# Bias tables of a neighbourhood attention loaded once per group in one transfer, into two buffers, a group ahead

## The chip, the core and the metric

The kernel runs on one core of a Trainium2 chip. The metric is the device time in microseconds (us) of one execution. The engines named below are TensorE (PE in the profile, its weight loads PEld), VectorE (DVE), ScalarE (ACT), GpSimd (POOL) and SyncE (SP). SP computes nothing here: it is the queue from which nearly all DMA transfers are issued, in a fixed order, each of them after the waits that it carries.

## What is computed

The program is a two-layer backbone over 1024 latent tokens (a grid of 16 rows by 64 columns) with 256 context tokens ahead of them. The first layer has two attentions, the second a convolution and a 2-D neighbourhood attention. The change lies in this second attention:

```python
bias = rpb[:, dr_idx][:, :, dc_idx] + col_mask[None, None]
bias = jnp.transpose(bias, (0, 2, 1, 3)).reshape(D_HEADS, GRID_W, kh * GRID_W)
bias = jnp.concatenate([ctx_open, bias], axis=-1)[None, :, None]
kk = jnp.concatenate([c_dk, kr], axis=1)
vv = jnp.concatenate([c_dv, vr], axis=1)
return gqa_attend(qr[:, :, :, None, :], kk, vv, bias).reshape(bsz, GRID_W, D_W)
```

Each of the 16 query rows sees a window of 8 key rows by 16 columns and the whole context; a learned table of relative positions is added to the scores. There are 8 heads of 64 channels. The host lays the table out for each head as additive tables with a large negative number where a key is outside the window.

## The kernel before

**Groups.** The second attention works in 16 groups: 8 heads times 2 halves of the grid's columns (`hf`; a half is 32 query columns by 16 rows, so 512 queries, and the 40 key columns that they can see, so 640 keys). `SEQ` sets the order of the groups: both halves of heads 0 to 5, then half 0 of heads 6 and 7, then half 1 of both. Below, group n is the n-th of this order, counted from 0.

**Tiles.** A group has 7 tiles of 128 keys: context, five tiles of grid keys, context. Only some query rows reach a key tile (`QROWS`), so the tiles are 512, 256, 352, 512, 320, 224 and 512 queries wide. `attn_gen` does for each tile: two matmuls for the scores (`st`, L467 and L471, keys on partitions), for grid tiles the addition of the bias on VectorE (`pf<-st,bs`, L476), the exponential on ScalarE, a split into two parts `ph` (ScalarE) and `pl` (GpSimd or VectorE), and, three tiles later, three matmuls with the values (`ov`, L411 to L413). At a group's end VectorE normalises, and `y` goes to DRAM (`O1d`, L1382).

**Preparation.** Ahead of its tiles a group is prepared by `attn_prep`: its queries are loaded (`QH` twice, `QL`, L1307 to L1309), the row maxima of the scores are found (`maxes`: matmuls `mx`, L1351 and L1359, then VectorE over `mx`, L1353, and over `mx` plus a second bias table with queries on partitions, `bm`, L1360), and the negated maxima are transposed (`trn`, L389) into a row of `QL`. Group g+2 is prepared while group g runs: its load is written at the start of group g, its `mx` some tiles later.

**Bias tables.** `bs` is the table that L476 adds. It is loaded piece by piece, one transfer for each grid tile, three tiles ahead (`ahead`, L1326), into one buffer for the 512-wide piece and four for the others. `bm` is the table for the maxima: three pieces for a group (440, 320 and 320 columns, L1316) in two buffers (`BMB = 2`), so that the third waits until the first is read. Every piece is a transfer of its own on SP's queue.

**Other loads of a group.** At the start of the first half of a head the keys of the next head are loaded (`KAt`, two transfers of 384 KB, L363), at the start of each group its values (`Vt`, two transfers, L1337), in its middle a gate (`gt`, L1331). `KAt` waits until the last score tile of the group before has been read by TensorE.

**What is woven in.** `weave` runs the attention with other work in turns: the projections of heads 4 to 7 (`p`, L320 to L322, with weights `wr`), then the output projection (`po`). These matmuls fill TensorE between an attention's tiles. The order of instructions on each engine, SP among them, is then set by a list scheduler from priorities, buffers and its own estimate of when things are ready. On the chip each engine keeps that order, whatever arrives late.

Of the kernel before, what the change touches and what calls it, by code (L numbers as in the profile page):

```python
# [10 lines left out]
F32 = mybir.dt.float32  # L11
# [7 lines left out]
P = 128  # L19
# [8 lines left out]
NR, NW = 16, 40  # L28
NCOL = (0, 24)
QROWS = ((0, 8), (0, 11), (0, 16), (6, 16), (9, 16))  # L30
KROWS = ((0, 8), (0, 11), (4, 15), (8, 16))
BSO = (0, 256, 608, 1120, 1440)
BMO = (0, 320, 320, 760)
LOOK0, LOOK1 = 3, 3
LEAD = (3, 4)
AHEAD = 3
BMB = 2
CWB = 12
VSH = 5
VORD = (1, 2, 0)  # L40
# [49 lines left out]
def tile_kernel(ctx: ExitStack, tc: tile.TileContext, a, out):  # L90
    nc = tc.nc
    VE, SC, GP, PE, SY = nc.vector, nc.scalar, nc.gpsimd, nc.tensor, nc.sync
# [20 lines left out]
    def nm(s):  # L113
        uid[0] += 1
        return f"{s}_{uid[0]}"
# [538 lines left out]
    with ExitStack() as p0x:  # L654
# [231 lines left out]
        for k in range(4):  # L886
            u = ORDER[k]
            n = NSTEP[u // 2] + (12 if k == 0 else 0)
# [216 lines left out]
    with ExitStack():  # L1105
# [182 lines left out]
        dpool = ctx.enter_context(tc.tile_pool(name="d1", bufs=1, reuse_waits="tile"))  # L1288
# [7 lines left out]
        def load_head(hd):  # L1296
            i, e = divmod(hd, 2)
            ds = slice(e * 64, (e + 1) * 64)
            heads[hd] = load_k(hd, KD[i][ds])

        def group1(gi, hd, hf):
            i, e = divmod(hd, 2)
            ds = slice(e * 64, (e + 1) * 64)
            bms, bss = {}, {}

            def load_q(QH, QL):
                SY.dma_start(QH[0:64, :].bitcast(F32), QD[i][ds, 0, hf])  # L1307
                SY.dma_start(QH[64:128, :].bitcast(F32), QD[i][ds, 0, hf])
                SY.dma_start(QL[0:64, :].bitcast(F32), QD[i][ds, 1, hf])  # L1309
                for b in (1, 0, 3):  # L1310
                    load_bm(b)

            def load_bm(b):
                n = (KROWS[b][1] - KROWS[b][0]) * NW
                bms[b] = dpool.tile([P, 440], F32, tag="bm", name=nm("bm"), bufs=BMB)[:, :n]
                SY.dma_start(bms[b], a["d_bm"][hd, hf, :, BMO[b] : BMO[b] + n])  # L1316
                if b == 1:
                    bms[2] = bms[1]

            def ahead(t):  # L1320
                if g.tiles[t][3] is not None:
                    n = g.tiles[t][2]
                    t -= 1
                    w = dpool.tile([P, 512 if n > 352 else 352], F32, tag="bsl" if n > 352 else "bss", name=nm("bs"),
                                   bufs=1 if n > 352 else 4)
                    SY.dma_start(w[:, :n], a["d_bs"][hd, hf, :, BSO[t] : BSO[t] + n])  # L1326
                    bss[t] = w[:, :n]

            def gate():
                g.gt = half("gt1")  # L1330
                SY.dma_start(g.gt[ds], GD[i][ds, hf])  # L1331

            def start():
                if hf == 0 and hd < 7:
                    load_head(hd + 1)
                for j, k, n in ((0, 0, 2), (2, 2 + 5 * hf, 5)):
                    SY.dma_start(Vs[gi % 2][:, j : j + n, 0:128].bitcast(F32), VD[i][:, k : k + n, e])  # L1337
# [34 lines left out]
            def finish(ov, rb):  # L1372
# [6 lines left out]
                if i == 3:  # L1379
                    split(y[ds], od3[hf][ds, 0], od3[hf][ds, 1], "s", "v")  # L1380
                    return
                SY.dma_start(O1d[ds, i, hf], y[ds])  # L1382

            g = Group(load_q=load_q, maxes=maxes, nmp=2, bias=True, rate=3, ahead=ahead, sink=None, tiles=tiles, den=den, finish=finish,
                      start=start, gate=gate, last=last,
                      k=lambda: Ks[hd % len(Ks)], load_v=None, v=lambda k: Vs[gi % 2][:, k if k < 2 else k - 5 * hf, :])
            g.prep = attn_prep(kvp, g)
            return g

        SEQ = [(hd, hf) for hd in range(6) for hf in range(2)] + [(hd, hf) for hf in range(2) for hd in (6, 7)]  # L1390
        groups1 = [group1(gi, *x) for gi, x in enumerate(SEQ)]
        load_head(0)
        copy_k(*heads[0])
# [249 lines left out]
```

## Time and profile before

| | |
|---|---|
| median of 3 runs | 1566.65 us |
| lowest, highest | 1564.84, 1571.33 us |
| span of the profiled execution, first to last instruction | 1569.6 us |
| mean granted TensorE clock in it | 0.961 |
| PE busy in the span | 1460.8 us (93%) |
| DVE, POOL, ACT busy | 1129.4, 830.0, 762.0 us |
| moved by DMA | 221.03 MB, mean 141 GB/s |
| first matmul of the second attention | 1219.29 us after the span's start |

For the profiled execution the profile gives the span and no second time around it; it lies 2.95 us above the median, inside the runs' own spread. The second attention runs from about 1219 us to about 1535 us of the span. A row of a timeline gives start and duration, then in brackets how long the engine had stood idle just before it and what ended that. A row of waits gives, for who waited and whom for, the sum in us, how many times, and the longest. Sizes in KB are those of the profile (1024 bytes).

### The profile page before, as it was taken

Reading aid. Unit: us, or ns where it says so; the run is one execution under the profiler, and the core shown is the slowest. Engines: PE = TensorE matmul, PEld = TensorE weight load, DVE = VectorE, ACT = ScalarE, POOL = GpSimd, SP = SyncE. Lnnn points to the kernel's source line nnn. Section 1 sums busy time; section 2 is a strip of 40 time slices with the busy share of each in tenths; the row PEclk is TensorE's granted clock in tenths of the full one; section 3 lists DMA queues with packets and bytes.
Section 4 is the critical chain, followed back from the end, with each engine's and each line's share of the span. In section 5 each row is a group of like instructions: output and inputs, shape, how many; then the busy total and the mean of one; then the engine's idle time right before and its main releaser. Section 6 shows DMA issues by size and latency. Waiting matters only on the chain.

```text
span 1569.6 us, 22251 instructions
## 1 busy us (share of the span) xinstructions
PE 1460.8 (93%) x6984; PEld 1178.9 (75%) x6984; DVE 1129.4 (72%) x2172; ACT 762.0 (49%) x1545; POOL 830.0 (53%) x762
## 2 busy tenths in 40 slices
PE   6989999998999999899999889999999999899995
PEld 1878877876888677588887568888887787677784
DVE  4898896797768677455488668999654466776776
ACT  2721354545454754655555746443343445545472
POOL 1561463555465675756545756665443333444575
PEclk9899999999999999999999989999999999799897
DMA  9548245424431225612112022214547888889632
GB/s 337 190 142 260 87 142 167 132 67 125 154 116 47 67 91 167 224 47 61 48 38 85 14 94 61 81 58 148 177 154 224 237 229 242 248 231 251 187 95 108
DMA packets 199438, 221.03 MB, mean 141 GB/s; under 512 B 18956, under 2 KB 155352, under 8 KB 199320
## 3 DMA queue, kind: packets, MB, share of 16 engines
q1 hardware_dynamic: 192656, 208.04, 43.5%
q10 hardware_dynamic: 6664, 11.57, 2.3%
q8 instruction: 55, 0.90, 0.2%
q14 instruction: 63, 0.52, 0.1%
HBM read 159.51 MB, written 60.03 MB: 140 GB/s over the span
## 4 chain that ended last, share of the span: by engine, by line
PE 65%; DVE 14%; DMA 11%; issue 4%; POOL 2%; SPq 2%; ACT 1%; ACTq 0%; DVEq 0%; POOLq 0%
PE p L322 6%; PE p L321 6%; PE p L320 6%; PE ov L411 4%; PE ov L413 4%; PE ov L412 4%; PE po L320 4%; PE po L321 4%; PE po L322 4%; PE st L467 4%; PE st L471 4%; DMA mw<-in_mod_w_dram 3%; DVE macc L221 2%; PE pq L322 2%; PE pq L321 2%
## 5 line engine op out<-in xcount | busy, mean ns | idle before, releaser
L301 POOL TENSOR_TENSOR pl<-pf,ph 128x512 fp32r<-128x512 f32 (+4 forms) x321 | 393.7, 1237 | 320.1 <-ACT ph L298 260.0
L301 POOL TENSOR_TENSOR wl<-wr,wh 128x256 fp32r<-128x256 f32 (+2 forms) x256 | 197.5, 788 | 203.1 <-ACT wh L298 192.4
L479 ACT ACTIVATE pf<-st 128x512 f32<-128x512 f32 x284 | 167.3, 597 | 177.4 <-PE st L471 138.3
L298 ACT CAST ph<-pf 128x512 fp32r<-128x512 f32 (+4 forms) x364 | 210.5, 588 | 28.9 <-PE ov L412 21.5
L298 ACT CAST wh<-wr 128x256 fp32r<-128x256 f32 (+2 forms) x264 | 102.8, 404 | 172.9 <-DMA wr<-in_ev_qkv_dram 40.4
L320 PE MATMUL p<-hh,wh 128*128 128x512 f32 x448 | 177.5, 398 | 2.9 <-DVE spk L301 1.5
L321 PE MATMUL p<-hl,wh 128*128 128x512 f32 x448 | 178.0, 398 | 0.2 <-POOL hl L301 0.2
L322 PE MATMUL p<-hh,wl 128*128 128x512 f32 x448 | 175.9, 400 | 0.1
L467 PE MATMUL st<-QH,KAt 128*128 128x512 f32 (+4 forms) x364 | 145.4, 401 | 11.4 <-ACT pf L479 9.7
L411 PE MATMUL ov<-ph,Vt 128*128 128x512 f32 (+4 forms) x364 | 143.5, 394 | 9.7 <-ACT ph L298 5.0
L413 PE MATMUL ov<-pl,Vt 128*128 128x512 f32 (+4 forms) x364 | 144.1, 396 | 6.8 <-POOL pl L301 3.6
L471 PE MATMUL st<-QL,KBt 68*128 68x512 f32 (+4 forms) x364 | 139.0, 391 | 5.8 <-DVE QL L390 5.7
L412 PE MATMUL ov<-ph,Vt 128*64 128x512 f32 (+4 forms) x364 | 140.5, 386 | 0.0
L1122 DVE SCALAR_TENSOR_TENSOR cps<-U,taps,cps 128x512 f32<-128x512 f32 x184 | 124.3, 748 | 0.0
L591 DVE TENSOR_REDUCE mp<-mx 128x1 f32<-128x512 f32 x128 | 85.7, 682 | 42.5 <-PE mx L590 41.8
L221 DVE SCALAR_TENSOR_TENSOR macc<-mw,csil,macc 128x512 f32<-128x512 f32 x107 | 94.5, 901 | 17.5 <-DMA mw<-in_mod_w_dram 16.7
L320 PEld LDWEIGHTS p<-hh,wh 128*128 128x128 f32 x448 | 84.6, 189 | 23.6 <-DVE spk L301 1.7
L321 PEld LDWEIGHTS p<-hl,wh 128*128 128x128 f32 x448 | 84.5, 189 | 20.4 <-POOL hl L301 0.6
L322 PEld LDWEIGHTS p<-hh,wl 128*128 128x128 f32 x448 | 84.8, 189 | 20.1 <-POOL wl L301 0.6
L467 PEld LDWEIGHTS st<-QH,KAt 128*128 128x128 f32 x364 | 71.2, 196 | 33.4 <-ACT pf L479 17.6
L413 PEld LDWEIGHTS ov<-pl,Vt 128*128 128x128 f32 x364 | 71.1, 195 | 32.5 <-POOL pl L301 7.8
L411 PEld LDWEIGHTS ov<-ph,Vt 128*128 128x128 f32 x364 | 71.3, 196 | 27.3 <-ACT ph L298 8.4
(277 smaller groups left out, 3546.2 us busy)
## 6 DMA issues: line engine op xcount, KB each, us to landing
mw<-in_mod_w_dram SPq DMA_DIRECT2D x34, 512.0 KB, 5.9
Q<-qs SPq DMA_DIRECT2D x40, 256.0 KB, 2.7
QH<-Q SPq DMA_DIRECT2D x80, 128.0 KB, 2.8
wr<-in_od_d_dram SPq DMA_DIRECT2D x64, 128.0 KB, 2.7
mw<-in_mod_w_dram SPq DMA_DIRECT2D x28, 256.0 KB, 3.3
wr<-in_ev_qkv_dram SPq DMA_DIRECT2D x32, 192.0 KB, 3.6
KAt<-KD SPq DMA_DIRECT2D x16, 384.0 KB, 6.2
wr<-in_od_wo_dram SPq DMA_DIRECT2D x48, 128.0 KB, 3.2
```

The costliest lines, as they stand in the source:

```text
L221: VE.scalar_tensor_tensor(t, w, csil[:, dk, q : q + 1], t, op0=ALU.mult, op1=ALU.add)
L298: SC.copy(hi, src)
L301: (GP if leng == "g" else VE).tensor_tensor(lo, src, hi.bitcast(F32), op=ALU.subtract)
L320: PE.matmul(o, lh, rh, start=first, stop=False)
L321: PE.matmul(o, lh, rl, start=False, stop=False)
L322: done[0] = PE.matmul(o, ll, rh, start=False, stop=last)
L411: PE.matmul(o, V[:, 64:192], ph[:, :n], start=(t == 0), stop=False)
L412: PE.matmul(g.ov[0:64, q0 : q0 + n], V[:, 0:64], ph[:, :n], start=False, stop=False)
L413: pvs.append(PE.matmul(o, V[:, 64:192], pl[:, :n], start=False, stop=(last and g.sink is None)))
L467: sts.append(PE.matmul(st[:, :n], KA[:, cs], g.QH[:, q0 : q0 + n], start=True, stop=False))
L471: PE.matmul(st[:, :n], KB[0:68, cs], g.QL[0:68, q0 : q0 + n], start=False, stop=True)
L479: SC.activation(pf[:, :n], st[:, :n], AF.Exp, scale=1.0 if g.bias else SCALE)
```

## The change

The two tables of a group are loaded whole. `bm` is one transfer of 128 x 1080 values (540 KB) in place of three, still written in `load_q`, into two buffers that hold a whole group. `bs` is one transfer of 128 x 1664 values (832 KB) in place of five, into two buffers as well; the load of group g+1 is written first in the start of group g (`load_bs`), and group 0 loads its own and that of group 1. `ahead` is left empty. The values and the arithmetic are the same, and so are the bytes: 5 x `bs` is 128 + 176 + 256 + 160 + 112 = 832 KB, 3 x `bm` is 220 + 160 + 160 = 540 KB.

```diff
-BMB = 2
+BSW, BMW = 1664, 1080
             def load_q(QH, QL):
                 SY.dma_start(QH[0:64, :].bitcast(F32), QD[i][ds, 0, hf])
                 SY.dma_start(QH[64:128, :].bitcast(F32), QD[i][ds, 0, hf])
                 SY.dma_start(QL[0:64, :].bitcast(F32), QD[i][ds, 1, hf])
-                for b in (1, 0, 3):
-                    load_bm(b)
-
-            def load_bm(b):
-                n = (KROWS[b][1] - KROWS[b][0]) * NW
-                bms[b] = dpool.tile([P, 440], F32, tag="bm", name=nm("bm"), bufs=BMB)[:, :n]
-                SY.dma_start(bms[b], a["d_bm"][hd, hf, :, BMO[b] : BMO[b] + n])
-                if b == 1:
-                    bms[2] = bms[1]
+                bm = dpool.tile([P, BMW], F32, tag="bm", name=nm("bm"), bufs=2)
+                SY.dma_start(bm, a["d_bm"][hd, hf])
+                for b in range(4):
+                    bms[b] = bm[:, BMO[b] : BMO[b] + (KROWS[b][1] - KROWS[b][0]) * NW]
 
             def ahead(t):
-                if g.tiles[t][3] is not None:
-                    n = g.tiles[t][2]
-                    t -= 1
-                    w = dpool.tile([P, 512 if n > 352 else 352], F32, tag="bsl" if n > 352 else "bss", name=nm("bs"),
-                                   bufs=1 if n > 352 else 4)
-                    SY.dma_start(w[:, :n], a["d_bs"][hd, hf, :, BSO[t] : BSO[t] + n])
-                    bss[t] = w[:, :n]
+                pass
+
+            def load_bs():
+                bs = dpool.tile([P, BSW], F32, tag="bs", name=nm("bs"), bufs=2)
+                SY.dma_start(bs, a["d_bs"][hd, hf])
+                for t, (r0, r1) in enumerate(QROWS):
+                    bss[t] = bs[:, BSO[t] : BSO[t] + (r1 - r0) * 32]
             def start():
+                for g2 in groups1[gi + 1 if gi else 0 : gi + 2]:
+                    g2.load_bs()
                 if hf == 0 and hd < 7:
                     load_head(hd + 1)
```

The scheduler places the instructions anew. On SP the 128 bias transfers of the second attention become 32. Here is SP's queue at the start of group 6, around the keys of head 4 (`KAt`) and the queries of group 8 (`QH_13996` before, `QH_13914` in the changed kernel; the last number of a name is a buffer). Before:

```order
L1316 DMA bm_13764<-in_d_bm_dram 128x320
L1326 DMA bs_13990<-in_d_bs_dram 128x512
L1316 DMA bm_14001<-in_d_bm_dram 128x440
L1326 DMA bs_14031<-in_d_bs_dram 128x320
L1244 DMA VD_7433<-spv_14564 128x512
L1382 DMA O1d<-y_3452_13849 64x512
L363 DMA KAt_12379<-KD_7428 64x1536 x2
L1307 DMA QH_13996<-QD_7424 64x512
L1308 DMA QH_13996<-QD_7424 64x512
L1309 DMA QL_13997<-QD_7424 64x512
L1316 DMA bm_14003<-in_d_bm_dram 128x320
L1326 DMA bs_14106<-in_d_bs_dram 128x224
```

In the changed kernel (`bm_14197` is the table of group 9, `bs_13908` that of group 7):

```order
L1311 DMA bm_14197<-in_d_bm_dram 128x1080
L331 DMA wr_14788<-in_od_wo_dram 128x256
L1379 DMA O1d<-y_3413_13771 64x512
L1244 DMA VD_7433<-spv_14454 128x512
L1320 DMA bs_13908<-in_d_bs_dram 128x1664
L363 DMA KAt_12379<-KD_7428 64x1536 x2
L1307 DMA QH_13914<-QD_7424 64x512
L1308 DMA QH_13914<-QD_7424 64x512
L1309 DMA QL_13915<-QD_7424 64x512
L1334 DMA Vt_12386<-VD_7431 128x2x128
L1334 DMA Vt_12386<-VD_7431 128x5x128
L331 DMA wr_14794<-in_od_wo_dram 128x256
```

What moved: two pieces of each table ahead of `KAt`, and more of them behind the queries, have become one whole `bs` right ahead of `KAt`; the `bm` of a group now stands well ahead of that group's own `QH` (here that of group 9 ahead of the queries of group 8).

The second place is TensorE at the end of group 6, between its last score tile and the first maxima of group 9. Before (the last score tile is `st_14246`, the maxima of group 9 read `QH_14286`):

```order
L467 MATMUL st_14246<-QH_13479,KAt_12382 128x512
L471 MATMUL st_14246<-QL_13480,KBt_12383 128x512
L1359 MATMUL mx_3559_14229<-KAt_12379,QH_13996 128x320
L1359 MATMUL mx_3560_14232<-KAt_12379,QH_13996 128x320
L411 MATMUL ov_14163<-ph_14145,Vt_12385 128x512
L412 MATMUL ov_14163<-ph_14145,Vt_12385 64x512
L389 MATMUL trn_14306<-ident,nmt_14256 4x128
L1351 MATMUL mx_3608_14427<-KAt_12379,QH_14286 128x256 x2
```

In the changed kernel the last score tile of group 6 is `st_14152`, and these rows stand right ahead of the maxima of group 9 (`QH_14192`), among them a score tile of group 7 (`QH_13685`):

```order
L413 MATMUL ov_14073<-pl_14156,Vt_12385 128x512
L389 MATMUL trn_14208<-ident,nmt_14162 4x128
L467 MATMUL st_14289<-QH_13685,KAt_12382 128x512
L471 MATMUL st_14289<-QL_13686,KBt_12383 128x512
L320 MATMUL po_3613_14526<-oc_14458,wh_14500 128x512
L321 MATMUL po_3613_14526<-oc_14458,wh_14500 128x512
L322 MATMUL po_3613_14526<-oc_14458,wl_14501 128x512
L320 MATMUL po_3613_14526<-oc_14458,wh_14506 128x512
L321 MATMUL po_3613_14526<-oc_14458,wh_14506 128x512
L322 MATMUL po_3613_14526<-oc_14458,wl_14507 128x512
L1348 MATMUL mx_3557_14325<-KAt_12379,QH_14192 128x256 x2
```

What moved: before, five rows of other work lie between the end of the last score tile and the maxima of group 9; in the changed kernel 31 rows do, most of them ahead of the rows shown.

More of the change, by code (lines that the diff above doesn't have):

```diff
@@ L1384, in group1 @@
             g = Group(load_q=load_q, maxes=maxes, nmp=2, bias=True, rate=3, ahead=ahead, sink=None, tiles=tiles, den=den, finish=finish,
-                      start=start, gate=gate, last=last,
+                      start=start, gate=gate, last=last, load_bs=load_bs,
                       k=lambda: Ks[hd % len(Ks)], load_v=None, v=lambda k: Vs[gi % 2][:, k if k < 2 else k - 5 * hf, :])
```

## The prediction

> **What bounds the kernel now.** First the page.
>
> ```profile
> span 1569.6 us, 22251 instructions
> PE 1460.8 (93%) x6984; PEld 1178.9 (75%) x6984; DVE 1129.4 (72%) x2172; ACT 762.0 (49%) x1545; POOL 830.0 (53%) x762
> PE 65%; DVE 14%; DMA 11%; issue 4%; POOL 2%; SPq 2%; ACT 1%; ACTq 0%; DVEq 0%; POOLq 0%
> ```
>
> TensorE sets the pace, and the chain that ended last leaves it for DVE and DMA. The change touches only the stretch from 1219 to 1535 us, so the busy time by stretch comes next (us, then busy time and count of each engine, granted clock, DMA share, GB/s).
>
> ```profile
> 1219.00:1290.00 71.00, 70.16 (x359) 58.37 (x360) 42.92 (x108) 32.81 (x72) 23.99 (x27) 0.98 0.80 229
> 1290.00:1314.00 24.00, 19.90 (x103) 15.97 (x102) 13.44 (x31) 12.94 (x29) 11.40 (x13) 1.00 0.90 249
> 1340.00:1370.00 30.00, 23.21 (x86) 17.16 (x86) 20.01 (x50) 15.75 (x34) 14.26 (x16) 0.72 0.88 250
> 1370.00:1440.00 70.00, 67.75 (x328) 54.03 (x326) 50.64 (x125) 35.68 (x73) 34.43 (x37) 1.00 0.86 241
> 1440.00:1480.00 40.00, 34.65 (x147) 27.47 (x147) 23.14 (x55) 17.44 (x37) 21.01 (x21) 0.87 0.78 210
> ```
>
> Matmuls per us are the honest measure. 1370 to 1440 runs 328/70 = 4.7 per us. At that pace the 86 matmuls of 1340 to 1370 need 18.3 us instead of 30 (11.7 lost), the 147 of 1440 to 1480 31.3 instead of 40 (8.7 lost), the 103 of 1290 to 1314 21.9 instead of 24 (2.1 lost). These 22.5 us are all that a better order of loads could win back in these stretches. DMA is busy at 0.78 to 0.90, so it matters what is loaded when. The waits say who is late (for whom, on whom: sum, times, longest).
>
> ```profile
> DVE mx L1360 <- DMA bm<-in_d_bm_dram: 14.1, 7, 3.2
> PE mx L1351 <- DMA QH<-QD: 9.0, 7, 3.2
> SPq L1326 <- DVE pf L476: 24.4, 23, 5.8
> SPq L1316 <- DVE mp L1360: 15.1, 15, 3.9
> ACT KBt L557 <- DMA KAt<-KD: 18.7, 7, 4.3
> ```
>
> DVE waits for a piece of `bm`, PE for the queries of a coming group, and ACT, which copies the keys, for `KAt`. SP itself stands at the `bs` pieces until a buffer is read, and everything behind them on SP stands too.
>
> **The change part by part.** *Fewer issues.* The rows by tile give the issue time on SP.
>
> ```profile
> L1326 SPq DMA_DIRECT2D bs<-in_d_bs_dram x80: 327/386/757, 1214.8 to 1509.4; - x80
> L1316 SPq DMA_DIRECT2D bm<-in_d_bm_dram x48: 327/381/1110, 1213.7 to 1482.4; - x48
> ```
>
> 128 issues become 32: 96 x 0.38 = 37 us less of SP's time. No instruction of PE waits for SP's issue alone; the cover is SP's own waits (24.4 + 15.1 us above). I count 0 here; without that cover it could give a few us.
>
> *The third piece of `bm`.* It waits for the first to be read, then travels; DVE stands still meanwhile (bracket: idle before, and why).
>
> ```profile
> 1346.61 0.50 DVE L1360 CUSTOM_DVE_ANT_0 mx<-mx,bm 128x320 f32<-128x320 f32 x1 [1.83 <-DMA bm<-in_d_bm_dram]
> 1363.30 0.50 DVE L1360 CUSTOM_DVE_ANT_0 mx<-mx,bm 128x320 f32<-128x320 f32 x1 [2.39 <-DMA bm<-in_d_bm_dram]
> 1433.62 0.50 DVE L1360 CUSTOM_DVE_ANT_0 mx<-mx,bm 128x320 f32<-128x320 f32 x1 [3.12 <-DMA bm<-in_d_bm_dram]
> 1477.19 0.50 DVE L1360 CUSTOM_DVE_ANT_0 mx<-mx,bm 128x320 f32<-128x320 f32 x1 [3.19 <-DMA bm<-in_d_bm_dram]
> ```
>
> In the new order a group's `bm` stands ahead of its own `QH`, in a buffer free since the maxima of two groups earlier, so these waits end. The first two fall into the worst stretch, where PE also runs at half clock:
>
> ```profile
> 1350.00:1355.00 5.00, 3.48 (x9) 2.11 (x9) 3.24 (x8) 3.13 (x6) 2.24 (x3) 0.50 1.04 241
> 1355.00:1360.00 5.00, 5.00 (x20) 4.37 (x19) 4.48 (x10) 0.90 (x3) 0.63 (x2) 0.56 0.90 237
> 1365.00:1370.00 5.00, 5.00 (x19) 4.34 (x18) 3.54 (x9) 2.99 (x7) 2.48 (x3) 0.54 0.54 158
> 1475.00:1480.00 5.00, 4.66 (x18) 3.64 (x16) 1.65 (x5) 2.60 (x6) 4.40 (x4) 0.66 0.79 224
> ```
>
> There little other work fills PE, and the DMA engines are full (1.04). Between 1341 and 1365 SP issues 6 pieces of `bm` and 8 of `bs`, some 2400 KB; the new order has one `bs` and one `bm` in that place, 1372 KB, because one `bs` and one `bm` more are already there. 1000 KB less at 241 GB/s is some 4.2 us of transfer, as an estimate. With the two waits (4.2 us) and about 2.3 us for the half clock that follows such stalls (5 us at 0.54 cost that much), bounds are 0 and 11.7; I take 7, as 4.2 and 4.2 overlap in part. The waits at 1433 and 1477 stand in front of PE gaps that are smaller than themselves:
>
> ```profile
> 1440.57 0.37 PE L467 MATMUL st<-QH,KAt 128*128 128x224 f32 x1 [0.78 <-DVE pf L476]
> ```
>
> 0.8 there and 1.7 from the clock at 1475 to 1480 (0.34 of 5 us) make 2.5; with the wait at 1399 not shown, I take 3, between 0 and 6.3 (their DVE waits).
>
> *`bs` ahead of `KAt` and `QH`.* This is the cost. 832 KB now stand right ahead of the keys. A transfer of this size in this stage is not in the trace: at the 353 GB/s of the fastest row below it would take 2.4 us, at the 245 of the other 3.5 us.
>
> ```profile
> 1305.00:1310.00 5.00, 5.00 (x30) 4.05 (x27) 1.11 (x2) 1.84 (x6) 1.93 (x2) 1.00 0.96 245
> 1320.00:1325.00 5.00, 5.00 (x25) 4.13 (x25) 4.86 (x11) 3.64 (x8) 1.39 (x2) 1.00 1.03 353
> ```
>
> But before, pieces stood there as well. SP at the start of group 4:
>
> ```profile
> 1302.18 1.02 SPq L1326 DMA_DIRECT2D bs<-in_d_bs_dram  x2
> 1303.77 0.86 SPq L1316 DMA_DIRECT2D bm<-in_d_bm_dram  x2
> 1304.72 1.09 SPq L363 DMA_DIRECT2D KAt<-KD  x2
> ```
>
> Two `bs` and two `bm`, by the order 256 + 160 + 220 + 160 = 796 KB within 3 us of `KAt`; at the start of group 6 the order shows 796 again. 832 against 796 costs 0.1 us. What is really late is `QH` behind `KAt`, and there PE stalls (chain: start, us, what; then PE):
>
> ```profile
> 1306.49 6.83 DMA QH<-QD
> 1331.65 3.22 DMA QH<-QD
> 1313.46 0.47 PE L1351 MATMUL mx<-KAt,QH 128*128 128x256 f32 x2 [3.16 <-DMA QH<-QD]
> 1452.16 0.77 PE L1351 MATMUL mx<-KAt,QH 128*128 128x256 f32 x2 [2.96 <-DMA QH<-QD]
> ```
>
> `QH` takes 6.83 us behind `KAt` and 3.22 without. This stays. The scheduler puts the `mx` later: between a group's last score tile and the `mx` of the group prepared behind it stand, summed over the starts of groups 1 to 10, 297 matmuls before and 423 now, 12.6 more each, 2.7 us at 4.7 per us. That covers a `bs` of 2.4 us. I take +0.5 us net; the bounds are -9.0 (all these stalls go) and +21 (6 heads x 3.5 us, nothing hidden).
>
> *A new wait.* `bs` of group g+1 needs the last read of `bs` by group g-1 on DVE; queued behind it on SP are `KAt` and `QH`. That read is at times late:
>
> ```profile
> 1359.77 0.39 PE L471 MATMUL st<-QL,KBt 68*128 68x512 f32 x1
> 1363.97 0.39 DVE L476 TENSOR_TENSOR pf<-st,bs 128x224 f32<-128x224 f32 x1
> 1465.72 0.40 PE L471 MATMUL st<-QL,KBt 68*128 68x512 f32 x1
> 1471.71 0.39 DVE L476 TENSOR_TENSOR pf<-st,bs 128x224 f32<-128x224 f32 x1
> ```
>
> PE has read the keys at 1360.2, DVE its bias at 1364.4: 4.2 us, and 6.0 at the second pair. Both belong to starts of groups without a `KAt`, where less stands in the queue, and the first is late because of the `bm` wait that goes. Taken as 0, up to +10.
>
> *Sum.* -7 - 3 + 0.5 + 0 = -9.5 us on the span of 1569.6, so 1560.1; the median is 2.95 lower. Carried to it: 1566.65 - 9.5 = **1557 us**.
>
> **The rivals.**
> (B) *The waits were covered.* DVE is 72% busy, its idle time may cost nothing, and the stall moves from `bm` to the next late load, `QH` or the values behind it. For: the PE gap at 1440 is a quarter of the 3.12 us wait. Against: 11.7 us are lost where two waits and full DMA meet. Gain 1 or 2: 1565 us.
> (C) *The whole `bs` holds up SP's queue.* `KAt` and `QH` wait both for DVE's last read and for 832 KB. From the point where this exceeds the 2.7 us that the order gave, PE stalls. The lags of 4.2 and 6.0 are the largest of 16 pairs whose positive ones sum to some 20 us; 6 heads x 3.0 (between 2.4 and 3.5) add 18; ten starts x 2.7 that the order covers take off 27: 11 left. Three stalls with a half-clock window of 1.7 behind them add 5, and only 3 of the 10 won at `bm` stay, since PE now waits for `QH` in the same places: 1566.65 + 16 - 3 = 1579 us. For: `QH` behind `KAt` already takes 6.83. Against: 796 KB stood there before. The Trainium skill ("DMA: Bandwidth & Descriptors", Queues, rings and completion order) says that each DMA engine takes descriptors in ring order, so a small transfer waits for all that was issued ahead; 6.83 against 3.22 agrees, and by that rule C's 3.0 us each are paid in full.
> (D) *Whole tables also move faster.* 16 x 1372 KB = 22.5 MB take 90 us at 250 GB/s and 64 at 353; 26 us of DMA time less would let the `QH` stalls (9.0) and one or two half-clock windows (3) go: 1557 - 12 = 1545 us. Against: in 1305 to 1310, with `KAt` in rows of 6 KB, DMA is full at 245 GB/s, and the 353 came with shorter rows. The Trainium skill ("Perfetto Trace Analysis", DMA Optimizations) holds larger transfers to be the faster ones; these two rows don't show it here.
> That the tables are not ahead at all is excluded by the order: `bs_13908`, issued at the start of group 6, is group 7's.
>
> **How the numbers follow.** Chances: forecast 0.45 (own range 1548 to 1562), B 0.20 (1560 to 1573), C 0.27 (1568 to 1590), D 0.08. The range 1545 to 1581 leaves out half of D and a quarter to a half of C, some 0.15. A measurement here tells about 0.5% (7.8 us) from no change: faster is below 1558.8, slower above 1574.5. Faster: most of the forecast and D, 0.42 + 0.08 = 0.50. Same: B, 0.03 of the forecast and 0.03 of C, 0.26. Slower: 0.24.
>
> **What would show it.** Right: no wait of L1360 on `bm`; the 86 matmuls of the worst stretch in some 23 us; waits of PE on `QH` still near 9 us; clock windows fewer. B: those DVE waits gone, and the lost time unchanged. C: long waits of SP at L1320 on DVE, `QH` landing 9 us or more after issue, PE waiting for it over 15 us in sum. D: GB/s above 300 in windows with `bs`. Wrong altogether if PE waits for `bs` or for the values, of which the trace before shows next to nothing.

## The result, and the profile after

| | median, us | lowest to highest, us | ratio to before, 95% |
|---|---|---|---|
| before, beside these runs | 1567.22 | 1564.84 to 1573.64 | |
| changed | 1559.37 | 1553.45 to 1564.48 | 0.9943 (0.9925 to 0.9962) |
| changed, once more (f1) | 1560.73 | 1556.73 to 1569.62 | 0.9971 (0.9950 to 0.9993) |

Each ratio is to the runs of before in the same batch. By the two ratios the changed kernel is faster by 0.3 to 0.6%, some 4.5 to 9 us. The forecast was 1557. Both medians lie in the forecast's own range (1548 to 1562), but 1559.37 is 0.6 us above the 1558.8 below which the prediction would call the kernel faster, and 1560.73 lies in rival B's range (1560 to 1573) as well. So the time alone does not tell the forecast from B; the profiles have to. The first lines of the changed kernel's page:

```profile
span 1559.3 us, 22034 instructions
PE 1453.3 (93%) x6984; PEld 1174.9 (75%) x6984; DVE 1124.3 (72%) x2172; ACT 763.1 (49%) x1545; POOL 828.7 (53%) x762
```

TensorE has the same 6984 matmuls; 217 other instructions are gone (22251 before). A row of waits gives, for who waited and on whom, the sum in us, how many times, and the longest. The waits of VectorE between 1215 and 1535 us show what became of the waits on `bm`. Line numbers are 3 lower than before: L1357 is the max over `bm`, L1350 the max over the first two blocks.

```profile
DVE pl L301 <- ACT ph L298: 20.7, 11, 4.7
DVE mx L1357 <- PE mx L1356: 18.2, 18, 3.9
DVE mp L1350 <- PE mx L1348: 17.4, 4, 9.3
```

No wait of VectorE on `bm` or `bs` is left. It waits for TensorE in their place. The same view of a second profile of the kernel before (run f2, below) shows how much one execution differs from another:

```profile
DVE mp L1353 <- PE mx L1351: 13.6, 4, 10.1
DVE mx L1360 <- DMA bm<-in_d_bm_dram: 12.9, 7, 3.1
DVE mx L1360 <- PE mx L1359: 9.8, 9, 2.4
```

The three rows of the maxima sum to 36.3 us there; the two rows that are left sum to 35.6 us after the change. The wait changed its name and kept its size.

TensorE's own waits on DMA, after the change:

```profile
PE mx L1348 <- DMA QH<-QD: 9.9, 6, 4.0
PE mx L1348 <- DMA KAt<-KD: 3.8, 2, 2.0
```

That is 13.7 us; in the changed kernel's second profile 6.7 and 2.5, together 9.2. The kernel before has 9.0 + 2.6 in its first profile and, in its second:

```profile
PE mx L1351 <- DMA QH<-QD: 7.7, 5, 2.8
PE mx L1351 <- DMA KAt<-KD: 7.0, 2, 4.5
```

Where did the gain come from? One caution first: where a profile's execution has a time of its own on record, that time is 1.8 us above the span (1561.07 and 1559.3 after). The first profile of before, with its span of 1569.6 us, is then the execution of 1571.33 us, the slowest of its three, 4.7 us above their median and not 2.95. Busy time by stretch, after the change (us, then busy time and count of each engine, granted clock, DMA share, GB/s):

```profile
1290.00:1314.00 24.00, 20.21 (x102) 16.11 (x100) 13.59 (x33) 11.65 (x25) 9.35 (x11) 0.99 0.93 244
1340.00:1370.00 30.00, 21.75 (x96) 16.00 (x94) 18.25 (x47) 16.30 (x35) 15.82 (x18) 0.83 0.91 247
1370.00:1440.00 70.00, 68.55 (x341) 56.31 (x341) 54.76 (x136) 38.23 (x78) 36.99 (x38) 1.00 0.86 254
1440.00:1480.00 40.00, 36.66 (x171) 29.41 (x170) 26.82 (x64) 20.12 (x42) 23.26 (x26) 0.96 0.75 208
```

and in the second profile of before:

```profile
1340.00:1370.00 30.00, 23.77 (x98) 17.82 (x97) 21.30 (x53) 15.74 (x33) 14.14 (x16) 0.83 0.89 247
1370.00:1440.00 70.00, 65.52 (x318) 52.56 (x317) 49.68 (x121) 35.39 (x73) 34.19 (x37) 1.00 0.84 237
1440.00:1480.00 40.00, 33.14 (x151) 25.72 (x150) 24.09 (x56) 16.53 (x35) 20.73 (x22) 0.96 0.76 201
```

In 1340 to 1370, the stretch on which the prediction's largest term lay, TensorE did 86 matmuls before, and 96 after; but the second execution of the kernel before did 98. Nothing was won there that the kernel before doesn't reach by chance. In 1440 to 1480 it is another matter: 147 and 151 before, 171 and 178 after. At 4.7 matmuls per us these 24 to 27 are some 5 us. The maxima of a new head's first group lie in this stretch. Here is their first matmul (start, duration, and in brackets the idle time before it and its releaser), first in the second profile of before:

```profile
1450.14 0.76 PE L1351 MATMUL mx<-KAt,QH 128*128 128x256 f32 x2 [4.46 <-DMA KAt<-KD]
```

and after the change:

```profile
1453.10 0.69 PE L1348 MATMUL mx<-KAt,QH 128*128 128x256 f32 x2 [2.03 <-DMA KAt<-KD]
```

The second profile after has 0.55 us there, the first before 2.96. The other place in this stretch is the wait on the third piece of `bm`, which is gone (in the second profile of before; the first has 3.19 us at 1477.19):

```profile
1473.68 0.50 DVE L1360 CUSTOM_DVE_ANT_0 mx<-mx,bm 128x320 f32<-128x320 f32 x1 [3.08 <-DMA bm<-in_d_bm_dram]
```

After the change the `mx` also stands a little later in TensorE's order: `st` L471 is right ahead of it, where before it was `ov` L413.

To see this for all runs but g3, TensorE's work was divided after the same counts of matmuls in each profile. The table gives the time that TensorE lost in each part: the time between the starts of its first and last matmul, less 0.233 us for each 512 columns that it multiplied (the spacing of such matmuls where the granted clock is 1.00). The parts end near 1291, 1375, 1440, 1480 and 1529 us; the last column is the time from there to the end of the span.

| profile | to 1291 | to 1375 | to 1440 | to 1480 | to 1529 | rest |
|---|---|---|---|---|---|---|
| before | 2.3 | 23.2 | 5.9 | 11.2 | 0.3 | 38.9 |
| before again (f2) | 1.2 | 20.8 | 6.9 | 10.8 | -0.1 | 38.9 |
| changed | 2.2 | 24.9 | 2.3 | 5.9 | 0.6 | 37.7 |
| changed again (f1) | 1.1 | 24.9 | 2.7 | 4.4 | 0.8 | 37.7 |
| `bm` whole alone (e1) | 1.0 | 19.8 | 8.0 | 7.5 | 0.1 | 39.0 |
| `bs` whole alone (e2) | 2.3 | 29.7 | 7.5 | 10.2 | 0.4 | 38.4 |
| six `bm` buffers (e3) | 2.3 | 24.5 | 4.8 | 6.1 | 0.5 | 41.2 |
| `bm` in three, whole buffers (f3) | 1.5 | 22.5 | 6.0 | 5.5 | -0.4 | 38.8 |
| changed, `bs` in five (e4) | 0.7 | 25.2 | 4.7 | 4.1 | 1.0 | 37.5 |
| changed, `bs` at the gate (f4) | 2.6 | 26.0 | 5.0 | 4.3 | 0.8 | 38.7 |
| before, maxes later (g1) | 2.0 | 21.8 | 5.9 | 8.7 | -0.3 | 39.1 |
| changed, maxes later (g2) | 0.5 | 21.1 | 5.3 | 4.1 | 0.5 | 38.4 |
| changed, no tables (g4) | 0.9 | 19.5 | 3.6 | 3.2 | 0.1 | 37.8 |

Means of two profiles each, changed less before: -0.1, +2.9, -3.9, -5.8, +0.6 and -1.2 us. The part to 1375, with the worst stretch in it, did not gain: it came out 2.9 us worse, where the two profiles of before differ by 2.4. The two parts behind it hold the gain. Two things limit such figures. The kernels order their matmuls differently, so the parts hold the same count of matmuls and not quite the same ones; parts that end a few matmuls earlier or later move a figure by some 1 us. And each row is one execution: the profiled one was 8.3 us slower than its kernel's median in e2 and 4.1 in f4, 2.3 slower in e1 and 3.7 faster in f3.

### The profile page after: what moved, and what is told of

Same layout as the page of the kernel before. It is cut to its first block, busy times and chain, and to the rows that moved or that the text cites. A ratio compares the mean times of both kernels' runs of the same rounds, so it can differ in the third digit from the quotient of the medians.

```text
span 1559.3 us, 22034 instructions
## 1 busy us (share of the span) xinstructions
PE 1453.3 (93%) x6984; PEld 1174.9 (75%) x6984; DVE 1124.3 (72%) x2172; ACT 763.1 (49%) x1545; POOL 828.7 (53%) x762
## 4 chain that ended last, share of the span: by engine, by line
PE 66%; DVE 13%; DMA 10%; issue 4%; POOL 3%; ACT 2%; SPq 2%; ACTq 0%; DVEq 0%; POOLq 0%
PE p L322 6%; PE p L320 6%; PE p L321 6%; PE ov L411 4%; PE ov L413 4%; PE ov L412 4%; PE po L320 4%; PE po L321 4%; PE po L322 4%; PE st L471 3%; PE st L467 3%; DMA QH<-QD 3%; PE pq L322 2%; PE pq L321 2%; PE pq L320 2%
## 5 line engine op out<-in xcount | busy, mean ns | idle before, releaser
L298 ACT CAST ph<-pf 128x512 fp32r<-128x512 f32 (+4 forms) x364 | 210.8, 588 | 30.9 <-PE ov L412 22.7
L467 PE MATMUL st<-QH,KAt 128*128 128x512 f32 (+4 forms) x364 | 143.3, 395 | 12.5 <-ACT pf L479 10.2
L413 PE MATMUL ov<-pl,Vt 128*128 128x512 f32 (+4 forms) x364 | 144.0, 396 | 6.4 <-POOL pl L301 6.4
L471 PE MATMUL st<-QL,KBt 68*128 68x512 f32 (+4 forms) x364 | 137.5, 387 | 5.7 <-DVE QL L390 5.6
L221 DVE SCALAR_TENSOR_TENSOR macc<-mw,csil,macc 128x512 f32<-128x512 f32 x107 | 95.3, 909 | 13.4 <-DMA mw<-in_mod_w_dram 12.3
L321 PEld LDWEIGHTS p<-hl,wh 128*128 128x128 f32 x448 | 84.7, 189 | 20.8 <-POOL hl L301 0.6
L322 PEld LDWEIGHTS p<-hh,wl 128*128 128x128 f32 x448 | 84.7, 189 | 20.5 <-POOL wl L301 1.0
L413 PEld LDWEIGHTS ov<-pl,Vt 128*128 128x128 f32 x364 | 70.5, 194 | 33.8 <-POOL pl L301 12.7
L411 PEld LDWEIGHTS ov<-ph,Vt 128*128 128x128 f32 x364 | 70.6, 194 | 23.2 <-ACT ph L298 5.3
```

What stands on the lines that cost most here:

```text
L298: SC.copy(hi, src)
L321: PE.matmul(o, lh, rl, start=False, stop=False)
L322: done[0] = PE.matmul(o, ll, rh, start=False, stop=last)
L411: PE.matmul(o, V[:, 64:192], ph[:, :n], start=(t == 0), stop=False)
L413: pvs.append(PE.matmul(o, V[:, 64:192], pl[:, :n], start=False, stop=(last and g.sink is None)))
L467: sts.append(PE.matmul(st[:, :n], KA[:, cs], g.QH[:, q0 : q0 + n], start=True, stop=False))
```

## The experiments

The times are medians; "before" in the three batches was 1568.33, 1567.41 and 1567.44 us, and each ratio is to the runs of before in the same batch. The waits are sums between 1215 and 1535 us of one profile each (to 1545 for g1 to g4): VectorE's at the maxima on `bm`, and on TensorE; TensorE's at `mx` on `QH` and `KAt`.

| run | us | ratio, 95% | on `bm` | on TensorE | on `QH`, `KAt` |
|---|---|---|---|---|---|
| before | | | 14.1 | 23.9 | 11.6 |
| before again (f2) | 1568.06 | 1.0016 (0.9995 to 1.0037) | 12.9 | 23.4 | 14.7 |
| `bm` whole alone (e1) | 1562.41 | 0.9956 (0.9937 to 0.9976) | 0 | 29.5 | 12.3 |
| `bs` whole alone (e2) | 1569.21 | 1.0014 (0.9996 to 1.0032) | 24.0 | 30.9 | 10.2 |
| six `bm` buffers (e3) | 1568.09 | 0.9993 (0.9975 to 1.0011) | 0 | 35.2 | 14.0 |
| `bm` in three, whole buffers (f3) | 1565.07 | 0.9994 (0.9972 to 1.0015) | 0 | 29.5 | 12.3 |
| changed, `bs` in five (e4) | 1562.61 | 0.9971 (0.9952 to 0.9990) | 0 | 33.0 | 9.7 |
| changed, `bs` at the gate (f4) | 1562.17 | 0.9979 (0.9962 to 0.9996) | 0.3 | 33.1 | 9.0 |
| changed again (f1) | 1560.73 | 0.9971 (0.9950 to 0.9993) | 0 | 37.1 | 9.2 |
| before, maxes later (g1) | 1567.25 | 0.9992 (0.9974 to 1.0010) | 6.7 | 30.8 | 8.8 |
| changed, maxes later (g2) | 1559.46 | 0.9955 (0.9933 to 0.9977) | 0 | 39.1 | 10.4 |
| changed, six more issues (g3) | 1585.50 | 1.0095 (1.0065 to 1.0126) | 0 | 41.4 | 14.8 |
| changed, no tables (g4) | 1553.40 | 0.9893 (0.9868 to 0.9917) | 0 | 26.0 | 4.7 |

### e1: `bm` whole, `bs` as before

```diff
             def ahead(t):
-                pass
...
-            def load_bs():
...
+                if g.tiles[t][3] is not None:
...
+                    SY.dma_start(w[:, :n], a["d_bs"][hd, hf, :, BSO[t] : BSO[t] + n])
```

(against the changed kernel: the pieces of `bs` come back.)

> The bm table alone whole, in two buffers; bs in pieces as before. If the gain of 0.57% comes from the waits of VectorE on bm (14.1 us in seven waits) and the half-clock windows behind them: ratio 0.994 to 0.997, no wait of L1360 on a bm transfer left, queries still landing about 4 us after their issue. If it comes from the bs tables being there a group ahead: ratio 0.998 to 1.002.

1562.41 us. The ratio, 0.9956, lies between the changed kernel's two, 0.9943 and 0.9971. So `bm` alone brings what the whole change brings, as far as these runs can tell. No wait on `bm` is left, and `QH` lands 4.9 us after its issue in the median, where the first theory asked for about 4.

### e2: `bs` whole and a group ahead, `bm` as before

```diff
-                    SY.dma_start(w[:, :n], a["d_bs"][hd, hf, :, BSO[t] : BSO[t] + n])
...
+                SY.dma_start(bs, a["d_bs"][hd, hf])
```

(against the kernel before.)

> The bs table alone whole, a group ahead; bm in three pieces and two buffers as before. Theory bm: ratio 0.999 to 1.005, waits of VectorE on bm as long as before or longer (14 us or more), because each piece of bm now travels behind a bs of 832 KB; the queries land later (median 6 us or more instead of 4.2). Theory bs: ratio 0.994 to 0.997.

1569.21 us, ratio 1.0014: nothing, or a slight loss. VectorE's waits on the pieces of `bm` grew, probably since a whole `bs` now stands in their way:

```profile
DVE mx L1363 <- DMA bm<-in_d_bm_dram: 24.0, 10, 5.0
DVE mx L1363 <- PE mx L1362: 18.0, 12, 3.2
```

24.0 us of such waits, 10 us more than before, while the time moved by 2 us (5 at most, by the end of its interval, 1.0032). The two don't stand in proportion, though the profile is of the slowest of twelve executions (1577.50 us), so its rows overstate the usual loss. One expectation was missed: `QH` lands 4.9 us after its issue in the median and not 6 or more. It is late mostly where the keys of a new head are loaded ahead of it (8.8, 8.2 and 8.9 us at 1268.8, 1306.3 and 1349.9 us, against 5.8, 6.8 and 6.5 in the first profile of before).

### e3: the kernel before with six buffers for the pieces of `bm`

```diff
-BMB = 2
+BMB = 6
```

> The kernel before with six buffers for the pieces of bm in place of two; nothing is merged. If the number of buffers is what counted, the third piece no longer waits for the first to be read: ratio as with the bm table whole (0.994 to 0.997). If the number of transfers on SP counted, the ratio stays at 0.998 to 1.002 although the waits on bm are gone.

1568.09 us, no change, with the wait gone: the outcome that the expectation ascribed to the number of transfers. VectorE's list starts with TensorE:

```profile
DVE mp L1353 <- PE mx L1351: 20.6, 8, 9.6
DVE mx L1360 <- PE mx L1359: 14.6, 11, 3.6
```

This is 35.2 us against 38.0 for the three kinds in the first profile of before. Taking the wait away, and nothing else, is worth 1 us in time, at best 4 by the interval (0.9975). The table by parts shows why it isn't more: up to 1440 us TensorE loses as much as before (31.6 us against 31.4 and 28.9), in the part to 1480 it loses 5 us less, and the rest behind 1529 us takes 41.2 us instead of 38.9, the longest in the table, with the last norms in another order. About half of what was won is given back there.

### e4: the changed kernel with `bs` in five transfers into the same buffer

```diff
-                SY.dma_start(bs, a["d_bs"][hd, hf])
...
-                    bss[t] = bs[:, BSO[t] : BSO[t] + (r1 - r0) * 32]
+                    n = (r1 - r0) * 32
+                    bss[t] = bs[:, BSO[t] : BSO[t] + n]
+                    SY.dma_start(bss[t], a["d_bs"][hd, hf, :, BSO[t] : BSO[t] + n])
```

> The changed kernel with bs loaded in five transfers into the same whole buffer, at the same place in the program: 64 transfers more on SP. If only buffers and lead counted: the same as the change, ratio to before 0.992 to 0.996. If the number of transfers on SP counted (64 x 0.38 = 24 us of SP's time): at least half of the gain is lost, 0.997 or more.

1562.61 us, ratio 0.9971. By the expectation this is just inside the range for "the number of transfers counted", but the changed kernel's second measurement has the same ratio, so one or five transfers for `bs` can't be told apart. In five pieces, at the same place in the program, `bs` does not hold up `QH` in the median: it lands 4.5 us after its issue.

### f1 and f2: the two kernels once more

> The changed kernel once more, for a second profile and for times in one batch with the others. 1556 to 1563 us, ratio .992 to .997. Theory A (the waits of DVE on the third piece of bm were what cost): no wait of DVE's max on bm, in this profile either. Rival B (the first pair of profiles differs mostly in how many half-clock windows fell into it): the sum of the half-clock windows between 1215 and 1535 us differs from the first profile's 20.5 us by 7 us or more, while the time stays.

> The kernel before once more, for a second profile. 1564 to 1571 us, ratio 0.998 to 1.002. Theory A: DVE waits for bm at its max near 14 us (10 to 18) again. Rival B: the half-clock windows of this profile are not the first profile's 34.1 us but lie between 17 and 48 us, and its span moves with them by half a us for each us.

The changed kernel's profile has no wait on `bm` in either execution. Before has 12.9 us, the range expected. The clock differs by execution, not by kernel: mean granted clock 0.961 and 0.967 in the two profiles of before, 0.966 and 0.964 after. The trace's half-clock windows (stretches with a granted clock of 0.5), counted from the first maxima to 1520 us, sum to 34.1 and 20.5 us before and 20.5 and 23.9 after. By the first pair alone one would have told a story of 13.6 us less at half clock, worth 6.8 us; by the second pair it is 3.4 us more. That story fell. Before, 13.6 us less at half clock went with a span 3.9 us shorter, where f2's rival B asked for 6.8. The half of f1 that asked for 7 us or more between the changed kernel's two profiles did not come about (3.4).

### f3: e1 with `bm` in three transfers, into the whole buffer

```diff
-                SY.dma_start(bm, a["d_bm"][hd, hf])
-                for b in range(4):
-                    bms[b] = bm[:, BMO[b] : BMO[b] + (KROWS[b][1] - KROWS[b][0]) * NW]
+                for b in (1, 0, 3, 2):
+                    n = (KROWS[b][1] - KROWS[b][0]) * NW
+                    bms[b] = bm[:, BMO[b] : BMO[b] + n]
+                    if b != 2:
+                        SY.dma_start(bms[b], a["d_bm"][hd, hf, :, BMO[b] : BMO[b] + n])
```

> e1_bm_only with bm's one transfer cut into the three of before, all into the whole buffer: no piece waits for a buffer. Theory A (the wait for the freed buffer was the price): as e1_bm_only, 1560 to 1565 us, no wait of DVE's max on bm above 2 us. Rival C (it is the number of transfers that SP issues and the DMA engines take): as e3_bm_six_buffers, 1566 to 1570 us. Rival N (each edit makes the scheduler reorder the stage, and the time moves by some us with the order alone): anything from 1559 to 1571 us without a row that answers for it.

The median fell between what theories A and C named, 1565.07 us, and the ratio is 0.9994. It is the second kernel without the wait and with three transfers, and the second whose ratio is one. e1, with one transfer, has 0.9956. The upper end of e1 (0.9976) just passes the lower ends of e3 and f3 (0.9975 and 0.9972), so that e1 is faster than those two by some 6 us is likely, and not beyond doubt. Whether the number of transfers does it or the new order of the instructions (rival N) these runs don't tell, for each edit changes both. The profile of f3 was taken of one of its quicker executions (span 1559.6 us, of a kernel that ran between 1557.84 and 1573.68 us), so its row in the table by parts flatters it.

### f4: `bs` of the next group issued in the middle of a group

```diff
             def start():
-                for g2 in groups1[gi + 1 if gi else 0 : gi + 2]:
-                    g2.load_bs()
+                if gi == 0:
+                    load_bs()
...
             def gate():
...
+                if gi + 1 < len(groups1):
+                    groups1[gi + 1].load_bs()
```

> The changed kernel with the next group's bs issued from the middle of the group, not at its start ahead of KAt and Vt. Theory Q (bs ahead of the latency-critical KAt and QH costs something): QH lands in a median below 6 us instead of 7.2, PE's waits for QH and KAt fall from 13.7 us to below 9, and the time from 1559 to 1554-1557 us. Rival H (that lateness is hidden): 1558 to 1562 us. Rival V (bs now comes late for its own reader, or holds up what is issued in the middle of the group): above 1563 us, with waits for bs on DVE or ACT.

The rows by tile give the time from issue to landing of `QH` (its second half, L1308). First the changed kernel, then f4:

```profile
L1308 SPq DMA_DIRECT2D QH<-QD x16: 444/596/972, 1081.8 to 1463.3; - x16
DMA to landing us min/median/max: 2.9/7.2/10.9
```

```profile
L1308 SPq DMA_DIRECT2D QH<-QD x16: 444/594/1254, 1084.0 to 1468.2; - x16
DMA to landing us min/median/max: 2.9/4.5/8.8
```

`QH` lands in 4.5 us in the median instead of 7.2 (4.2 before). The rows one by one say where: at 1268.8 and 1306.2 us the scheduler still put `bs` right ahead of `KAt`, and `QH` took 8.8 and 8.1 us; at 1347.9, with `bs` out of the way, 4.4, where the changed kernel has 9.1. So a whole `bs` ahead of `KAt` does make `QH` late there. TensorE's wait for `QH` and `KAt` is 9.0 us, as in the better of the two profiles of the changed kernel (13.7 and 9.2), and the time is no better: 1562.17 us, just past rival H's range and short of rival V's. That this lateness is hidden, as H says, fits; the move of `bs` changed the order of the other instructions too, so a small gain and a small loss may also have met.

### g1 and g2: the maxes of a group one tile later

```diff
-LEAD = (3, 4)
+LEAD = (3, 5)
```

once in the kernel before (g1), once in the changed one (g2).

> The kernel before, with the maxes of a group taken up one tile later (LEAD 5 for 4), and nothing of the change. Theory O (a good part of the change's gain is the order: the new group's mx stands behind more matmuls, so that KAt and QH have landed when PE gets there): the mx that ended the 3 to 4.5 us stall near 1450 us stalls under 1.5 us, and the time falls by 2 to 6 us to 1562-1566. Theory A (waits on bm): they stay near 13 us and the time stays at 1566-1569. Rival L (later maxes come late for DVE's nmt and the st behind it): 1570 us or more.

> The changed kernel with the maxes one tile later (LEAD 5 for 4). Theory O: PE's waits for QH and KAt (13.7 and 9.2 us in the two profiles) fall below 6 us, and the time from 1560 to 1555-1558 us. Theory A and rival H (that lateness is hidden): 1559 to 1562 us. Rival L: above 1563 us.

1567.25 and 1559.46 us: no change from either. Theory O, as put, fell: in g1 the stall near 1450 us was still 2.17 us, in g2 TensorE's waits on `QH` and `KAt` stayed at 10.4 us, and its time is the one that theory A and rival H named. g1 says something else, though. Its waits on `bm` are halved, to 6.7 us: those of the worst stretch and the 3 us near 1432 are gone, the first and the one near the end are left.

```profile
1471.35 0.50 DVE L1360 CUSTOM_DVE_ANT_0 mx<-mx,bm 128x320 f32<-128x320 f32 x1 [3.04 <-DMA bm<-in_d_bm_dram]
```

Its loss to 1375 us (21.8) is that of before (23.2 and 20.8): the waits of the worst stretch cost nothing that shows here. Theory A had the time right and the waits wrong. And its loss from 1440 to 1480 is 8.7 us, between before (11.2, 10.8) and the changed kernel (5.9, 4.4).

### g3: six more transfers of 4 KB a group

```diff
+                g.xt = dpool.tile([P, 48], F32, tag="xt", name=nm("xt"), bufs=2)
+                for x in range(2):
+                    SY.dma_start(g.xt[:, x * 8 : x * 8 + 8], a["d_bm"][hd, hf, :, x * 8 : x * 8 + 8])

             def ahead(t):
-                pass
+                if g.tiles[t][3] is not None and t > 1:
+                    x = t
+                    SY.dma_start(g.xt[:, x * 8 : x * 8 + 8], a["d_bm"][hd, hf, :, x * 8 : x * 8 + 8])
```

> The changed kernel with six more transfers a group, of 8 columns each (4 KB) into a buffer that nothing reads: as many issues as before, nearly no bytes. Theory C (number of transfers is what bm in one transfer won over bm in three): 1564 to 1567 us, back towards before. The prediction's term (fewer issues are worth 0): 1559 to 1562 us.

1585.50 us: 25 us more than the changed kernel, beyond any theory. SyncE's order shows where it starts (start, duration, the instruction and its count):

```profile
1239.03 1.59 SPq L331 DMA_DIRECT2D wr<-in_od_d_dram  x3
1240.68 0.90 SPq L1316 DMA_DIRECT2D xt<-in_d_bm_dram  x2
1241.63 0.90 SPq L1321 DMA_DIRECT2D xt<-in_d_bm_dram  x2
1242.57 0.91 SPq L1316 DMA_DIRECT2D xt<-in_d_bm_dram  x2
1243.51 1.57 SPq L1321 DMA_DIRECT2D xt<-in_d_bm_dram  x3
1245.19 0.47 SPq L1311 DMA_DIRECT2D bm<-in_d_bm_dram  x1
...
1250.55 0.88 SPq L331 DMA_DIRECT2D wr<-in_od_d_dram  x2
```

Nothing reads these transfers, so nothing holds them back: the scheduler put all 96 between 1215 and 1349 us, not spread over sixteen groups. SyncE issues them one after the other at some 0.43 us each. The weights `wr` of 1250.55 us stand behind them, 10 us after the load of `wr` before; ScalarE, which splits the weights, stands idle for 7.97 us until they land, and TensorE waits for ScalarE:

```profile
1254.13 0.79 PE L320 MATMUL p<-hh,wh 128*128 128x512 f32 x1 [5.09 <-ACT wh L298]
```

By parts as in the table, TensorE loses some 8 us more than in the changed kernel up to 1291 us, some 10 more in the next part, and the rest behind. So issues on SyncE are not free here where they stand ahead of loads that TensorE is about to need. What the 96 issues that the change saves were worth where they stood, this run doesn't say.

### g4: the tables left out

```diff
-                bm = dpool.tile([P, BMW], F32, tag="bm", name=nm("bm"), bufs=2)
-                SY.dma_start(bm, a["d_bm"][hd, hf])
+                if gi < 2:
+                    TB["m", gi] = dpool.tile([P, BMW], F32, tag="bm", name=nm("bm"), bufs=2)
+                    SY.dma_start(TB["m", gi], a["d_bm"][hd, hf])
+                bm = TB["m", gi % 2]
```

and the same for `bs`.

> The changed kernel with bm and bs loaded for the first two groups only and used again by the others, so the transfers of 14 of the 16 groups' tables (19 MB) are left out. An upper bound on what any way of loading them can still win. If the tables' traffic still holds up QH, KAt or the weights: under 1554 us, QH landing in a median below 4.5 us. If all of it is hidden (rival H): 1557 to 1561 us.

1553.40 us, ratio 0.9893 (0.9868 to 0.9917): 17 us below before by the ratio, 14 by the medians. The kernel leaves out the tables of 14 groups, whose scores get the tables of the first two. As far as the order of the instructions doesn't matter, this is about what any way of loading the tables could win; the change takes 4.5 to 9 us of it. Under 1554 us, with `QH` landing in 3.0 us in the median, is what was expected if the tables' traffic still holds up other loads. TensorE's waits for the queries and the keys shrink and don't vanish:

```profile
PE mx L1353 <- DMA KAt<-KD: 3.2, 2, 1.9
PE mx L1353 <- DMA QH<-QD: 1.5, 3, 0.8
```

4.7 us instead of 9.2 and 13.7 in the changed kernel, so about half of this wait or more is the tables' doing, by one profile.

No version that loads all its tables beats the changed kernel; g2 equals it.

## Why the prediction came out as it did

The first median came within 3 us of the forecast and the second within 4. The steps did not all hold, and the largest one failed.

- **Fewer issues, counted 0.** Not settled. SyncE's waits did cover them: before it stood at `bs` for VectorE, after it stands at the weights for GpSimd (24.9 us before). One row of SyncE's waits after, between 1200 and 1535 us:

```profile
SPq L331 <- POOL wl L301: 56.4, 43, 5.6
```

  The time that SyncE gained became waiting time. But e1 against e3 and f3 leaves room for a gain from one transfer in place of three, and g3 shows that issues in the full part of the queue are far from free, as the clause "without that cover it could give a few us" allowed.

- **The third piece of `bm`, -7 in the worst stretch.** This is the step that failed. The waits went, but nothing was won there: 24.9 us are lost to 1375 us in both profiles after, 23.2 and 20.8 before. Four runs take the same waits away without `bs` ahead, and lose 19.8 (e1), 24.5 (e3), 22.5 (f3) and 21.8 (g1): 22.2 us in the mean, where before has 22.0. The working took 4.2 us of VectorE's waits, with the half clock behind them, for time of the kernel. In their place stood VectorE's wait for TensorE's `mx`: 35.6 and 37.1 us after the change, where the three kinds of wait together had 38.0 and 36.3 before. The 86 matmuls were to take 23 us. The changed kernel did 96 in the 30 us, 10 more, worth 2.1 us at 4.7 per us, and the second profile of before did 98. Rival B had this step right.

- **The third piece of `bm`, -3 at the waits behind.** The mechanism holds as far as the parts show it; the size is between 2.6 and 5.2 us. Four profiles have a wait of 3 us or more on this piece between 1471 and 1481 us: the two of before, e2 and g1. They lose 8.7 to 11.2 us in the part to 1480. The nine that have none lose 3.2 to 7.5. The difference of means is 5.2 us (10.2 and 5.0). Half of that goes with the clock: in this part the trace has 10.2, 3.4, 6.8 and 3.4 us at half clock in these four, 3.4 in the first profile after and in e1, none in the other seven. With half of each taken off, the means are 7.3 and 4.6, and the lowest of the four (6.1, the first profile of before) is level with the highest of the nine (6.1, e3). It isn't the wait's alone either: the stall at the new head's first `mx` lies in the same part (2.96 and 4.46 us before, 2.03 and 0.55 after), and the order that each edit makes anew takes part in it. e1 still has 2.04 us there, with 7.5 us lost in all. And the 5 us that e3 gains in this part did not reach its time.

- **`bs` ahead of `KAt` and `QH`, +0.5.** Right as a sum, within what the runs can tell: e2 gives +2 us (-0.6 to +5), and e1 and the changed kernel don't differ. What it is the sum of stays open. To 1375 us the six profiles with `bs` a group ahead lose 21.1 (g2) to 29.7 us (e2, its slowest execution), 25.3 in the mean; the six without it, g4 aside, 19.8 to 24.5, 22.1 in the mean. From there to 1440 us it is the other way: 4.6 against 6.3 us, with ranges that overlap again (2.3 to 7.5 and 4.8 to 8.0). So `bs` may cost some 3 us first and give some 2 back. `QH` lands 3 us later in the median (4.2 to 7.2), as the estimate of 2.4 to 3.5 us for one `bs` had it. The rule of the Trainium skill ("DMA: Bandwidth & Descriptors", Queues, rings and completion order) agrees with the landing, 9.1 us behind `bs` and 4.4 us without it at the same place in f4; that each such delay is paid in full, as rival C would have it, no run shows. Of C's signs one came in part: at three starts of a head `QH` landed 9.1 to 10.9 us after its issue. TensorE's waits for it stayed at 9.9 and 6.7 us, not above 15, and SyncE waited under 4 us at L1320 for VectorE. (C's own sum is 1579.65 us, which the prediction gives as 1579.)

- **`QH` waits stay near 9 us.** Right: 9.0 and 7.7 before, 9.9 and 6.7 after.

- **A new wait on `bs`, 0.** Right for the wait that was meant: no wait on `bs` is in the lists of TensorE and VectorE, and SyncE's wait for VectorE's last read is not among its longest. Another one is new. SyncE has waits that the profile puts down to a transfer of `bs` still on its way, 15.3 and 13.9 us in sum in the two profiles after, 2.1 and 1.8 before. What they cost no run shows.

- **Whole tables move faster (rival D).** Its sign, windows above 300 GB/s, does not tell the kernels apart. The four stretches above show 208 to 254 GB/s; in windows of 5 us between 1215 and 1535 both kernels pass 300, in 9 and 7 windows before and in 12 and 9 after, at most 356 before and 418 after. The Trainium skill ("Perfetto Trace Analysis", DMA Optimizations) holds larger transfers to be the faster ones. The runs don't decide: 254 against 241 and 237 GB/s in 1370 to 1440 us is 5 to 7% more at the same or a slightly higher DMA share, and the time is not D's 1545 us.

In sum: -7 came to nothing, -3 came to between -2.6 and -5.2 by the parts, and the part from 1375 to 1440 us (-3.9) and the rest behind 1529 us (-1.2) gave what the prediction had not put there. That the sum came out near -9.5 is largely luck: without its failed term the prediction stands at -2.5, near rival B's gain of 1 or 2 us, and the measured gain lies between the two.

Open is what makes `bm` in one transfer (e1) better in time than three without waits (e3, f3). Candidates are the two issues a group that it saves and the scheduler's order; in e3 the rest behind 1529 us, with the last norms in another order, takes 2.3 us longer. So the waits alone (e3, f3) don't account for the gain in time, and its cause is found only down to "`bm` whole". An order held fixed by hand over both forms of `bm` wasn't tried.

## What to carry to other kernels

A wait in the trace is worth what the bounding engine loses in that part, not its own length. Here the waits on one table could go without any gain that shows, but for the one near the end, which went with 3 to 5 us of TensorE's time together with its neighbour. A count of lost time by parts of the same work showed this, and the sums of waits didn't. Leave the traffic out altogether once (here 14 to 17 us): that says about how much there is to win, and how much a change has taken of it. And where executions of one kernel spread by 9 us or more, a second profile of each kernel is needed before a stretch or a clock window is given as the cause.

## What the runs showed that was not expected

- 96 transfers of 4 KB, 0.4 MB together, cost 25 us, more than the 19 MB of tables that g4 leaves out (6 us by the medians between the changed kernel and g4, 8 to 12 by the ratios). They came in a bunch ahead of weights, 0.43 us of SyncE each.
- The time at half clock differs by execution: 34.1 and 20.5 us for the same kernel with the same order of instructions, in steps of 3.4 us, in most profiles near the same places (1220, 1315, 1350 to 1365 and 1453 us).
